# Attention score matmuls with 128 rows throughout: the queries' remainders in zero-padded tiles

## Chip, cores and metric

One core of one Trainium2 chip (trn2). The metric is the device time of the program in microseconds (us), the median over runs of the same kernel on the chip. PE stands for TensorE's matmuls, PEld for its weight loads, DVE for VectorE, ACT for ScalarE, POOL for GpSimd, SP for SyncE.

## What is computed

Two layers of a transformer over 512 latent tokens (and 256 context tokens) of width 1024, in float32: feed-forward, mixer, feed-forward. The mixer of layer 0 is a pooling one, that of layer 1 is a differential attention with 8 heads, each with two halves of 64 columns. Only the attention is touched here:

```python
def proj(h):                      # queries, keys: 8 heads x 2 halves x 64; values: 8 heads x 128
    q, k, v = jnp.split(h @ w_qkv, 3, axis=-1)
...
def attend(q, k, v):
    s = jnp.einsum('bqhjd,bkhjd->bhjqk', q, k).astype(jnp.float32) * scale
    p = jax.nn.softmax(s, axis=-1)
    a = p[:, :, 0] - lam_full * p[:, :, 1]
    return jnp.einsum('bhqk,bkhe->bqhe', a.astype(v.dtype), v)
```

The 512 latent queries see 768 keys (latents and context). Each of the two halves of a head has its own scores and its own softmax; the second softmax is subtracted from the first.

## The kernel before

Everything that goes through TensorE is float32 split into a high part and a rest (type fp32r), so that a product of two numbers takes three matmuls: high by high, high by rest, rest by high (`mm3`, L556 to L559). A weight's item of 512 columns is cast by ACT (L155) and its rest is taken by DVE (L156), six items ahead of their use.

The program runs in stages: feed-forward, pooling, feed-forward, feed-forward, attention, feed-forward with the final norm. The attention (L1170 to L1481) goes through 32 steps s, four blocks of 128 queries for each of the 8 heads, written out as a loop at L1437. Step s puts this on the queues, in this order: `combine(s-1)`, which joins the two softmaxes of the step before on DVE (L1302); three transposes of the joined block of step s-2 on PE (L1324), which ACT and DVE split again (L1326, L1327); `score(s, 0)`; three more transposes; `score(s, 1)`; then pieces of other work that a table spreads over the steps (projections of queries, keys and values of later heads, named `pj`; the output projection `yo`); and, in odd steps, the product with the values (`pv`).

`score(s, j)` (L1281) makes the scores of half j of a head for 128 queries and 768 keys, in two matmul pairs of 384 keys. The contraction has only 64 rows, and the other 64 of the 128 partitions carry the keys' rest: `k0` holds the high part of half 0's keys in partitions 0 to 63 and their rest in 64 to 127, `k1` the other way round (`k_split`, L1216). `q0` and `q1` hold the queries' high part twice. So one 128-row matmul (L1291) gives high by high plus high by rest. The queries' own rest lies in one tile `ql`, half 0 in partitions 0 to 63, half 1 in 64 to 127 (L1241, L1242), and a second matmul with 64 rows (L1292) multiplies it with the keys' high part:

```python
nc.tensor.matmul(o, q[:, qs], k[:, ks], start=True, stop=False)
lately["pe"] = nc.tensor.matmul(o, ql[rows, qs], k[rows, ks], start=False, stop=True).ins
```

There are 64 such scores, so 128 matmuls of each line. What follows a score: DVE takes the maximum (L1294, L1295), ACT the exponentials with their sums (L1298). Scores lie in two PSUM tiles used in turn. The queries are turned by `rope` (L1198), whose two POOL operations (L1205, L1206) stand ahead of the split of the queries (L1237 to L1242) and of the keys (L1219 to L1222).

`sT` (L87), the silu of the conditioning vectors, is 1 KB in each partition of a pool that lives through the whole program; it is read in the modulation vectors' matmuls and sums (L391, L398).

Of the kernel before, what the change touches and what calls it, by code (L numbers as in the profile page):

```python
# [11 lines left out]
F32 = mybir.dt.float32  # L12
F32R = mybir.dt.float32r
# [5 lines left out]
P = 128  # L19
D = 1024  # L20
KD = D // P
NL = 512
# [10 lines left out]
# how far the weights' items, their raw tiles and the units of the vectors' weights run ahead  # L33
# [3 lines left out]
# vectors that the tensor engine does as a whole; vectors done by the end of each stage; units between other work  # L37
# [12 lines left out]
class Half:  # L50
    """Half of the tokens in the order lat, ctx; segs: (residual tile, first column, columns, conditioning, offset)."""
# [8 lines left out]
def dit_kernel(ctx: ExitStack, tc: tile.TileContext, a: dict, out: bass.AP):  # L60
    nc = tc.nc
# [25 lines left out]
    sT = base.tile([P, KD, 32], F32, name="sT")  # L87
# [19 lines left out]
    # ---------------------------------------------------------------- weight stream  # L107
    # Raw tiles come by DMA; items of 512 columns are split from them into a high part and the rest, in the order
    # in which the tensor engine asks for them.
# [55 lines left out]
    def weights(key, keep=False):  # L165
        """The two parts of an item; the splitting of the following ones is emitted first."""
        n = item_of[key]
        issue(n + 1 + (AHEAD if state["ahead"] else 0))
        return split[n] if keep else split.pop(n)
# [7 lines left out]
    sums = {}  # L177

    def pre(c, which):
        """Sums of the four blocks of a chunk (gate, up) x (first, second half of d)."""  # L180
        def f(raws):
            g, u = raws[0], raws[1]
            g0, g1, u0, u1 = g[:, 0:512], g[:, 512:1024], u[:, 0:512], u[:, 512:1024]
            if which == "S1":
                return sums.pop((c, "S1"))
            t = stemp()
            if which == "S2":
                s1 = stemp()
                nc.gpsimd.tensor_add(s1, u0, u1)  # L189
                sums[(c, "S1")] = s1  # L190
                nc.gpsimd.tensor_sub(t, s1, g0)
                sums[(c, "S2")] = t
                return t
            if which == "S3":
                nc.gpsimd.tensor_sub(t, g0, u0)
                return t
            nc.gpsimd.tensor_sub(t, g1, sums.pop((c, "S2")))  # L197
            return t
        return f
# [39 lines left out]
    def plan_cols(key, w, rows):  # L239
        """Items of two row blocks by 256 columns each."""  # L240
        for m in range(0, rows, 4):
            r = raw_job(lambda t, m=m: nc.sync.dma_start(
                t[:, 0:256 * min(4, rows - m)].rearrange("p (k f) -> p k f", f=256), w[:, m:min(m + 4, rows)]))
            for e in range(min(4, rows - m) // 2):
                add_item(key + (m // 2 + e,), [r], half(e))
# [10 lines left out]
    # products: weights block, normed block  # L256
# [24 lines left out]
    # ---------------------------------------------------------------- background work, drained between matmuls  # L281
# [11 lines left out]
    # ---------------------------------------------------------------- modulation vectors  # L293
# [37 lines left out]
    class Ada:  # L331
        """The vectors' weights come as units of 128 rows and 512 columns. A vector's products with the two rows of
        silu are either summed over the units first, per partition, so that the tensor engine has only the sums of
        the partitions left, or are the tensor engine's as a whole."""
# [15 lines left out]
        def room(self, u):  # L350
            """The tag that takes unit u: the sums' places take one too as long as no sum is near."""
# [54 lines left out]
        def tick(self, count):  # L406
            """The next units, up to the limit."""
# [29 lines left out]
        def until(self, n):  # L437
            """Vectors that are to be through before the next limit."""
            self.limit = n * 2 * KD
# [9 lines left out]
    # ---------------------------------------------------------------- norms  # L449
# [14 lines left out]
    def norm_square(pool, h, k, eng):  # L464
        """Adds chunk k of x*x to the half's accumulator; the last one is kept apart."""
# [12 lines left out]
    def rstd_of(pool, st, nb, count):  # L478
        """1/sqrt(mean + eps) of sums that lie with the tokens on the partitions."""
# [16 lines left out]
    def spread(diag, ps, nb):  # L496
        """Tokens from the partitions to the free axis, the same on every partition."""
        nc.tensor.matmul(ps[:, 0:nb * P], ones, diag[:, 0:nb * P], start=True, stop=True)

    def stat_steps(pool, bank, h, keep=True):  # L500
        """The two steps of a half's norm; other matmuls may go between them."""
# [26 lines left out]
    def scaled(pool, h, k, l, i, dst):  # L528
        """x * rstd * g * (1 + scale), before the shift."""
# [14 lines left out]
    def direct(pool, h, k, l, i, place, t=None):  # L544
        """Both parts of the modulated chunk; place(seg) says where they go."""
# [15 lines left out]
    # ---------------------------------------------------------------- feed-forward  # L561
    class FFN:
        """x += gate/2 * swiglu(hn), in chunks of 128 hidden units that are summed into x two at a time.

        Gate and up of a chunk are the two row blocks of a 2x2x2 block product (halves of d, halves of the tokens),
        done with seven block products (Strassen-Winograd) instead of eight."""
# [11 lines left out]
        # normed blocks and their sums  # L578
# [16 lines left out]
        def first_half(self, k):  # L595
            """Plain blocks of the first half; their values before the split are kept for the sums."""
# [16 lines left out]
        def pair_mod(self, j):  # L613
            """Modulated second half of d chunks j, j+4."""
# [7 lines left out]
        def pair_first(self, j):  # L622
            """The second half's blocks that the plain products of d chunks j and j+4 need, and T3."""
# [17 lines left out]
        # seven products of a chunk  # L641
# [12 lines left out]
        def use(self, c, name, ps):  # L654
            """What follows a product; t, u, s, v: running sums of chunk c."""
# [43 lines left out]
        # second product  # L699
        def y_k(self, b, k, h, c0):  # L700
            """Sum k into x for the tokens of h, which lie from column c0 on."""
# [33 lines left out]
        def first(self, lead, between=None, each=None):  # L735
            """Chunks 0 and 1, block by block; lead() brings the second half's norm on its way. between() goes between
            the two chunks' products of the first half; each(j) brings the first half's d chunks j and j+4. Returns
            what comes last."""
# [96 lines left out]
        def finish(self, each, steps, halves=None):  # L835
            """The last sum into x, half by half; each(half, k, m) follows a chunk's sum. steps: the two steps of the
            first half's norm, given once that half is through; what they queue is drained behind the chunks."""
# [15 lines left out]
    # ---------------------------------------------------------------- start  # L853
# [8 lines left out]
    fp1 = stage.enter_context(tc.tile_pool(name="fp1", bufs=1, reuse_waits="tile"))  # L862

    class Both:
        """Tiles of the feed-forward phases: fp1 from the start on, fp2 once the start is through."""
# [12 lines left out]
    with tc.tile_pool(name="st", bufs=1, reuse_waits="tile") as st:  # L878
# [10 lines left out]
        # rows k of the d blocks; columns j, j+4 of shift and of scale  # L889
# [10 lines left out]
        def more(n):  # L900
            """The next n loads of tokens and of the first two vectors' weights, in the order of need."""
# [92 lines left out]
    # ---------------------------------------------------------------- layer 0 and the first half of layer 1  # L994
# [10 lines left out]
    # pooling mixer, each token set with zeros on both sides  # L1005
# [101 lines left out]
    def lead(f, m, keep=True, queue=True):  # L1107
        """The steps of half m's norm for f; the first half's blocks are queued behind them."""
# [33 lines left out]
    # the normed tokens for the attention, lat then ctx  # L1142
    hn = {}
# [26 lines left out]
    # ---------------------------------------------------------------- differential attention  # L1170
# [45 lines left out]
    def k_split(kt, src, cols):  # L1216
        """Keys of both halves of a head: each half as high part and rest, one on top of the other."""
# [7 lines left out]

    def piece_q(h):
        qt = [ap.tile([P, NL], F32R, name=f"q{n}", tag=f"q{n}", bufs=2) for n in range(3)]
# [6 lines left out]
    def split_q(h):  # L1234
        t1 = turned.pop((h, 0))
        q0, q1, ql = qkt[h][0]
# [4 lines left out]
        nc.vector.tensor_sub(ql[LO_], t1[LO_], q0[LO_].bitcast(F32))  # L1241
        nc.vector.tensor_sub(ql[HI_], t1[HI_], q1[HI_].bitcast(F32))  # L1242
# [33 lines left out]
    def later(f, *args):  # L1276
        """f's work behind the latest scores and softmax."""
# [3 lines left out]
    def score(s, j):  # L1281
        h, qt = divmod(s, 4)
        qs = slice(qt * P, (qt + 1) * P)
        rows = (LO_, HI_)[j]
        (q0, q1, ql), (k0, k1) = qkt[h]
        q, k = ((q0, k0), (q1, k1))[j]
        sc = pp.tile([P, 2, 512], F32, name="sc", tag="sc", bufs=2)
        for half in range(2):
# [3 lines left out]
            lately["pe"] = nc.tensor.matmul(o, ql[rows, qs], k[rows, ks], start=False, stop=True).ins  # L1292
# [9 lines left out]
    def combine(s):  # L1302
        """p0 - lambda Z0/Z1 p1; the division by Z0 is part of the norm that follows the weighted sum."""
# [41 lines left out]
    def sub_rstd(ha, hb):  # L1345
        """osum <- 1/sqrt(mean(o*o) + eps*Z0*Z0) for heads ha..hb-1, o taken before the division by Z0."""
# [136 lines left out]
    # ---------------------------------------------------------------- last feed-forward, final norm  # L1483
# [15 lines left out]
    def turn(g, q, b):  # L1499
        """Quarter q of the rows of block b of the half, as token-major columns."""  # L1500
# [7 lines left out]
    def gained(g, b, half):  # L1508
        """The columns times the gain, before the row's factor."""
# [95 lines left out]
```

## Time and profile before

| | before |
|---|---|
| median of 3 runs (lowest to highest) | 2545.51 us (2544.54 to 2546.41) |
| span of the profiled execution | 2547.6 us |
| mean granted TensorE clock | 0.979 of full speed |
| PE busy | 2448.8 us (96%) |
| PEld busy | 2283.7 us (90%) |
| DVE busy | 2251.2 us (88%) |
| ACT busy | 1053.1 us (41%) |
| POOL busy | 698.2 us (27%) |
| DMA | 240.95 MB, 95 GB/s on average |

The page gives the span of the profiled execution, from its first to its last instruction, and no other time of that execution; the span stands 2.1 us above the median of the runs. A matmul's row begins when the instruction is taken up, and its length includes the time in which it is in the pipe, so that rows of neighbours overlap: what a matmul costs is read from the distance between the starts of neighbours. A PE that is busy throughout is therefore not a PE at its peak.

### The profile page before, as it was taken

What the parts mean: (1) busy time and instruction counts of PE and PEld (TensorE: products, weight loads), DVE (VectorE), ACT (ScalarE), POOL (GpSimd) and SP (SyncE); (2) the same over time, 40 slices, a digit from 0 to 9 for tenths busy, and PEclk for the clock granted to TensorE, in tenths of its full rate; (3) what the DMA queues carried; (4) which work ended last, traced back from release to release, by engine and by line L of the source; (5) the groups of instructions that cost most, each with busy time, mean ns of one, the idle gap of its engine ahead of it and who ended that gap; (6) DMA issues with size and microseconds to landing.
All of it is one profiled execution on the core that took longest, in us unless ns stands there. A gap on an engine that the chain in (4) does not pass through costs nothing.

```text
span 2547.6 us, 41218 instructions
## 1 busy us (share of the span) xinstructions
PE 2448.8 (96%) x15159; PEld 2283.7 (90%) x15159; DVE 2251.2 (88%) x4094; ACT 1053.1 (41%) x2082; POOL 698.2 (27%) x556
## 2 busy tenths in 40 slices
PE   8999999998899999999899999999999999899998
PEld 5899999996689999999899999998787778899998
DVE  5998999998998889989899999997777777899998
ACT  4533333334543333334533323335555554544444
POOL 0422222225432222222422222222312201433332
PEclk7999999998899999999999999999999999999999
DMA  9434333333323233333123334331111112232332
GB/s 265 124 104 120 104 112 121 112 116 108 96 65 106 84 99 92 100 108 91 50 86 118 112 108 121 116 92 59 50 38 38 34 34 83 67 96 88 100 100 67
DMA packets 314822, 240.95 MB, mean 95 GB/s; under 512 B 11293, under 2 KB 278910, under 8 KB 314622
## 3 DMA queue, kind: packets, MB, share of 16 engines
q1 hardware_dynamic: 314336, 238.20, 31.4%
q8 instruction: 121, 1.98, 0.3%
q14 instruction: 79, 0.65, 0.1%
q10 hardware_dynamic: 286, 0.12, 0.0%
HBM read 236.18 MB, written 2.10 MB: 94 GB/s over the span
## 4 chain that ended last, share of the span: by engine, by line
PE 64%; DVE 22%; issue 6%; DMA 4%; ACT 3%; POOL 2%; DVEq 0%; ACTq 0%; SPq 0%; POOLq 0%
PE prod L558 10%; PE prod L557 10%; PE prod L559 10%; PE y L557 6%; PE y L558 6%; PE y L559 6%; DVE asum L402 5%; DVE wlo L156 4%; DMA wrs<-in_ffn_w_out 3%; DVE hn L542 2%; PE sc L1292 2%; DVE xl L711 2%; DVE tmp L692 1%; PE pj L557 1%; PE sc L1291 1%
## 5 line engine op out<-in xcount | busy, mean ns | idle before, releaser
L558 PE MATMUL prod<-hn,whi 128*128 128x384 f32 (+1 forms) x2496 | 810.6, 325 | 17.3 <-DVE hn L542 17.2
L557 PE MATMUL prod<-hn,whi 128*128 128x384 f32 (+1 forms) x2496 | 808.6, 326 | 9.7 <-ACT hn L541 7.8
L559 PE MATMUL prod<-hn,wlo 128*128 128x384 f32 (+1 forms) x2496 | 809.0, 324 | 2.8 <-DVE wlo L156 2.7
L558 PEld LDWEIGHTS prod<-hn,whi 128*128 128x128 f32 x2496 | 475.7, 191 | 23.0 <-DVE hn L542 22.3
L557 PEld LDWEIGHTS prod<-hn,whi 128*128 128x128 f32 x2496 | 474.0, 191 | 24.0 <-ACT hn L541 11.5
L557 PE MATMUL y<-h_hi,whi 128*128 128x384 f32 (+2 forms) x1408 | 463.5, 329 | 24.4 <-DVE tmp L669 13.7
L559 PEld LDWEIGHTS prod<-hn,wlo 128*128 128x128 f32 x2496 | 475.5, 191 | 4.9 <-DVE wlo L156 4.1
L558 PE MATMUL y<-h_lo,whi 128*128 128x384 f32 (+2 forms) x1408 | 459.9, 327 | 5.2 <-DVE h_lo L542 5.1
L559 PE MATMUL y<-h_hi,wlo 128*128 128x384 f32 (+2 forms) x1408 | 456.4, 324 | 0.0
L155 ACT CAST whi<-ws 128x512 fp32r<-128x512 f32 x320 | 195.4, 619 | 485.9 <-PE y L558 361.1
L711 DVE SCALAR_TENSOR_TENSOR xl<-y,mT,xl 128x384 f32<-128x384 f32 (+3 forms) x688 | 311.8, 481 | 17.6 <-PE y L559 17.4
L402 DVE SCALAR_TENSOR_TENSOR asum<-araw,sT,asum 128x512 f32<-128x512 f32 x364 | 317.6, 885 | 0.4 <-ACT asum L400 0.2
L197 POOL TENSOR_TENSOR ws<-wraw,ws 128x512 f32<-128x512 f32 x80 | 111.6, 1394 | 728.3 <-DVE wlo L156 728.3
L557 PEld LDWEIGHTS y<-h_hi,whi 128*128 128x128 f32 x1408 | 266.7, 190 | 45.0 <-DVE tmp L669 18.9
L156 DVE TENSOR_TENSOR wlo<-wraw,whi 128x512 fp32r<-128x512 f32 x336 | 282.4, 845 | 23.7 <-ACT whi L155 23.2
L558 PEld LDWEIGHTS y<-h_lo,whi 128*128 128x128 f32 x1408 | 265.9, 189 | 10.9 <-DVE h_lo L542 9.1
L155 ACT CAST whi<-wraw 128x512 fp32r<-128x512 f32 x340 | 205.0, 617 | 164.0 <-PE y L558 61.1
L559 PEld LDWEIGHTS y<-h_hi,wlo 128*128 128x128 f32 x1408 | 266.2, 189 | 2.0 <-issue 0.5
L156 DVE TENSOR_TENSOR wlo<-ws,whi 128x512 fp32r<-128x512 f32 x320 | 247.8, 775 | 9.4 <-ACT whi L155 7.8
L189 POOL TENSOR_TENSOR ws<-wraw 128x512 f32<-128x512 f32 x80 | 114.1, 1426 | 396.7 <-DMA wraw<-in_ffn_w_in 317.5
L156 DVE TENSOR_TENSOR wlo<-wrs,whi 128x512 fp32r<-128x512 f32 x176 | 144.3, 822 | 62.4 <-ACT whi L155 62.0
L155 ACT CAST whi<-wrs 128x512 fp32r<-128x512 f32 x176 | 106.8, 618 | 196.6 <-DMA wrs<-in_ffn_w_out 160.8
(257 smaller groups left out, 3632.9 us busy)
## 6 DMA issues: line engine op xcount, KB each, us to landing
wraw<-in_ffn_w_in SPq DMA_DIRECT2D x176, 512.0 KB, 4.0
araw<-in_ada_w SPq DMA_DIRECT2D x246, 256.0 KB, 2.7
wrs<-in_ffn_w_out SPq DMA_DIRECT2D x176, 256.0 KB, 3.1
wraw<-in_diff_w_qkv SPq DMA_DIRECT2D x24, 512.0 KB, 3.7
hn<-in_ada_w SPq DMA_DIRECT2D x32, 256.0 KB, 5.3
asum<-in_ada_w SPq DMA_DIRECT2D x10, 256.0 KB, 2.8
hn<-in_x SPq DMA_DIRECT2D x8, 256.0 KB, 3.6
wraw<-in_diff_w_o SPq DMA_DIRECT2D x4, 512.0 KB, 4.0
```

The source lines that it names most:

```text
L155: nc.scalar.copy(hi, src)
L156: (nc.gpsimd if n in by_pool else nc.vector).tensor_sub(lo, src, hi.bitcast(F32))
L189: nc.gpsimd.tensor_add(s1, u0, u1)
L197: nc.gpsimd.tensor_sub(t, g1, sums.pop((c, "S2")))
L402: nc.vector.scalar_tensor_tensor(to, raw, by, to, op0=ALU.mult, op1=ALU.add)
L542: (eng or nc.vector).tensor_sub(dst[1], src, dst[0].bitcast(F32))
L557: nc.tensor.matmul(ps, whi, hi, start=start, stop=False)
L558: nc.tensor.matmul(ps, whi, lo, start=False, stop=False)
L559: nc.tensor.matmul(ps, wlo, hi, start=False, stop=stop)
L692: nc.vector.tensor_mul(up, up, gate)
L711: self.latest = nc.vector.scalar_tensor_tensor(x[:, k, t0:t0 + n], ps[:, off:off + n], mT[self.l][:, self.gate_v, k, cond:cond + 1], x[:, ...
L1292: lately["pe"] = nc.tensor.matmul(o, ql[rows, qs], k[rows, ks], start=False, stop=True).ins
```

## The change

The queries' rest gets a tile of its own for each half of a head: `l0` has half 0's rest in partitions 0 to 63 and zeros in 64 to 127, `l1` zeros below and half 1's rest above. Two pairs of such tiles serve the heads in turn. Their zero halves are written once, by four POOL memsets at the beginning of the attention, and only the other halves are written again for each head. The second matmul of a pair then uses all 128 rows of the padded tile and of the keys' tile; the zeros remove the keys' rest. `sT` moves into a pool that ends with the feed-forwards before the attention. Comments are taken out as well, so lines in the changed kernel stand one lower up to the attention and five or six higher in it.

```diff
-    sT = base.tile([P, KD, 32], F32, name="sT")
...
     fp1 = stage.enter_context(tc.tile_pool(name="fp1", bufs=1, reuse_waits="tile"))
+    sT = fp1.tile([P, KD, 32], F32, name="sT")
...
+    rests = [[apool.tile([P, NL], F32R, name=f"ql{j}{m}") for j in range(2)] for m in range(2)]
+    for pair in rests:
+        nc.gpsimd.memset(pair[0][HI_].bitcast(F32), 0.0)
+        nc.gpsimd.memset(pair[1][LO_].bitcast(F32), 0.0)
+
     def piece_q(h):
-        qt = [ap.tile([P, NL], F32R, name=f"q{n}", tag=f"q{n}", bufs=2) for n in range(3)]
+        qt = [ap.tile([P, NL], F32R, name=f"q{n}", tag=f"q{n}", bufs=2) for n in range(2)] + rests[h % 2]
...
-        q0, q1, ql = qkt[h][0]
+        q0, q1, l0, l1 = qkt[h][0]
...
-        nc.vector.tensor_sub(ql[LO_], t1[LO_], q0[LO_].bitcast(F32))
-        nc.vector.tensor_sub(ql[HI_], t1[HI_], q1[HI_].bitcast(F32))
+        nc.vector.tensor_sub(l0[LO_], t1[LO_], q0[LO_].bitcast(F32))
+        nc.vector.tensor_sub(l1[HI_], t1[HI_], q1[HI_].bitcast(F32))
...
-        rows = (LO_, HI_)[j]
-        (q0, q1, ql), (k0, k1) = qkt[h]
-        q, k = ((q0, k0), (q1, k1))[j]
+        (q0, q1, l0, l1), (k0, k1) = qkt[h]
+        q, ql, k = ((q0, l0, k0), (q1, l1, k1))[j]
...
-            lately["pe"] = nc.tensor.matmul(o, ql[rows, qs], k[rows, ks], start=False, stop=True).ins
+            lately["pe"] = nc.tensor.matmul(o, ql[:, qs], k[:, ks], start=False, stop=True).ins
```

The order of PE's instructions stays. This is PE in step 2 of the attention before, the transposes and the two scores of a step (sizes are those of the output, so the 64 rows of L1292 do not show in them):

```order
L1324 MATMUL atr<-ident,p 128x128 x3
L1291 MATMUL sc<-k_18696,q_18693 128x384
L1292 MATMUL sc<-k_18696,q_18695 128x384
L1291 MATMUL sc<-k_18696,q_18693 128x384
L1292 MATMUL sc<-k_18696,q_18695 128x384
L1324 MATMUL atr<-ident,p 128x128 x3
L1291 MATMUL sc<-k_18697,q_18694 128x384
L1292 MATMUL sc<-k_18697,q_18695 128x384
```

And the same place in the changed kernel:

```order
L1329 MATMUL atr<-ident,p 128x128 x3
L1296 MATMUL sc<-k_18703,q_18701 128x384
L1297 MATMUL sc<-k_18703,ql_18530 128x384
L1296 MATMUL sc<-k_18703,q_18701 128x384
L1297 MATMUL sc<-k_18703,ql_18530 128x384
L1329 MATMUL atr<-ident,p 128x128 x3
L1296 MATMUL sc<-k_18704,q_18702 128x384
L1297 MATMUL sc<-k_18704,ql_18531 128x384
```

Every second matmul of a pair reads one of two padded tiles where both read the one tile of the rest before; nothing stands elsewhere.

On POOL, at the seam between the feed-forward and the attention, four instructions are new. In brackets stand the engines that an instruction waits for. Before:

```order
L476 TENSOR_TENSOR acc<-acc,tmp 128x256 [waits Activation_49,Pool_49] x4
L1205 TENSOR_TENSOR t_18730<-t_18730,sin_t 128x512 [waits DVE_49,DMAHW6_49,PE_49,Activation_49]
L1206 TENSOR_TENSOR t_18731<-t_18731,t_18730 128x512 [waits PE_49,Pool_49]
L1239 TENSOR_SCALAR q_18693<-t_18731 64x512 [waits Pool_49]
L1240 TENSOR_SCALAR q_18694<-t_18731 64x512
```

And in the changed kernel:

```order
L475 TENSOR_TENSOR acc<-acc,tmp 128x256 [waits Activation_49,Pool_49] x4
L1229 MEMSET ql_18530 64x512 [waits DVE_49,PE_49,Pool_49]
L1230 MEMSET ql_18531 64x512
L1229 MEMSET ql_18532 64x512
L1230 MEMSET ql_18533 64x512 [waits DVE_49]
L1205 TENSOR_TENSOR t_18737<-t_18737,sin_t 128x512 [waits DVE_49,DMAHW6_49,Activation_49,Pool_49]
L1206 TENSOR_TENSOR t_18738<-t_18738,t_18737 128x512 [waits Pool_49]
L1245 TENSOR_SCALAR q_18701<-t_18738 64x512 [waits Pool_49]
```

The memsets stand between the last sum of squares of the stage before and the first rope multiplication, and take over a wait for PE that this multiplication had. On DVE and ACT the order is unchanged.

## Rows read from the trace of the kernel before

**Rows 1.** The page, part 4: the chain that ended last, share of the span by engine.

```profile
PE 64%; DVE 22%; issue 6%; DMA 4%; ACT 3%; POOL 2%; DVEq 0%; ACTq 0%; SPq 0%; POOLq 0%
```

**Rows 2.** Stretches of the attention: engines' busy us (instructions), PE clock, DMA share, GB/s.

```profile
core 0: us, PE busy (x) PEld busy (x) DVE busy (x) ACT busy (x) POOL busy (x), PEclk, DMA share, GB/s
1791.10:1822.20 31.10, 29.51 (x135) 21.20 (x134) 26.51 (x51) 19.07 (x37) 9.09 (x6) 0.92 0.18 53
...
1833.80:1883.90 50.10, 50.10 (x279) 39.72 (x277) 39.01 (x77) 28.67 (x59) 16.23 (x12) 1.00 0.14 41
1883.90:1917.50 33.60, 33.60 (x216) 28.11 (x213) 19.91 (x40) 14.65 (x31) 0.00 (x0) 1.00 0.12 35
...
2001.20:2054.90 53.70, 53.70 (x288) 41.17 (x285) 44.73 (x86) 28.69 (x59) 17.00 (x12) 1.00 0.10 30
...
2065.00:2112.10 47.10, 47.10 (x258) 36.24 (x257) 35.28 (x73) 25.83 (x52) 0.00 (x0) 1.00 0.15 45
```

**Rows 3.** Weight loads of the scores, 1788 to 2110 us: busy, mean ns, idle before, releasers.

```profile
L1291 PEld LDWEIGHTS sc<-k,q 128*128 128x128 f32 x128 | 24.5, 191 | 14.0 <-issue 12.2 <-ACT p L1298 0.7 <-DVE k L1221 0.4
...
L1292 PEld LDWEIGHTS sc<-k,q 64*128 64x128 f32 x128 | 23.8, 186 | 25.1 <-issue 25.1
```

**Rows 4.** Timeline of PE in step 10: start us, length us, instruction.

```profile
1883.64 0.49 PE L1324 MATMUL atr<-ident,p 128*128 128x128 f32 x3
1883.89 0.42 PE L1291 MATMUL sc<-k,q 128*128 128x384 f32 x1
1884.24 0.44 PE L1292 MATMUL sc<-k,q 64*128 64x384 f32 x1
1884.62 0.44 PE L1291 MATMUL sc<-k,q 128*128 128x384 f32 x1
1884.99 0.44 PE L1292 MATMUL sc<-k,q 64*128 64x384 f32 x1
1885.36 0.55 PE L1324 MATMUL atr<-ident,p 128*128 128x128 f32 x3
1885.66 0.42 PE L1291 MATMUL sc<-k,q 128*128 128x384 f32 x1
...
1887.12 0.39 PE L1268 MATMUL pj<-whi,hn 128*128 128x256 f32 x1
1887.34 0.28 PE L1269 MATMUL pj<-wlo,hn 128*128 128x256 f32 x1
1887.46 0.29 PE L1270 MATMUL pj<-whi,hn 128*128 128x256 f32 x1
```

**Rows 5.** Timeline of PE in a feed-forward: first and last of 14 neighbours.

```profile
1599.66 0.34 PE L558 MATMUL y<-h_lo,whi 128*128 128x384 f32 x1
...
1601.93 0.34 PE L559 MATMUL y<-h_hi,wlo 128*128 128x384 f32 x1
```

**Rows 6.** Timeline of POOL at the seam to the attention; in brackets idle time and releaser.

```profile
1748.93 4.64 POOL L476 TENSOR_TENSOR acc<-acc,tmp 128x256 f32<-128x256 f32 x5 [3.53 <-ACT tmp L462]
1779.56 1.49 POOL L1205 TENSOR_TENSOR t<-t,sin_t 128x512 f32<-128x512 f32 x1 [25.99 <-PE pj L1270]
...
1784.06 1.80 POOL L1240 TENSOR_SCALAR q<-t 64x512 fp32r<-64x512 f32 x1
```

**Rows 7.** The same columns as rows 2, a feed-forward and the pooling stage.

```profile
598.00:660.00 62.00, 48.97 (x377) 33.09 (x377) 53.80 (x99) 30.23 (x62) 31.06 (x27) 0.73 0.46 141
...
1500.00:1600.00 100.00, 98.37 (x566) 95.37 (x565) 99.41 (x176) 34.93 (x67) 25.85 (x17) 1.00 0.39 117
```

**Rows 8.** PE in step 3: the wait (timeline) and the stretch behind it (columns of rows 2).

```profile
1813.38 0.88 PE L1324 MATMUL atr<-ident,p 128*128 128x128 f32 x6 [1.15 <-DVE mx L1295]
...
1820.00:1824.00 4.00, 4.00 (x16) 3.01 (x14) 1.36 (x3) 1.27 (x4) 0.00 (x0) 0.50 0.02 4
```

## Prediction

> **What bounds the kernel now.** I read the page's chain first: PE carries 64% of what ended last, DVE 22% [rows 1]. That is a mean over the stages, so the attention is read by itself, in stretches [rows 2]. From the first score (1791 us) to the end of the last score's step (2112 us) PE is busy for the whole of every stretch but the first, while DVE has between 19.91 of 33.60 us (59%) and 26.51 of 31.10 us (85%). PE is the bound there, and a microsecond taken from PE comes off the end as long as DVE keeps up.
>
> What does PE do in that time? The weight loads show it: of the 128 loads of the 64-row matmuls each follows idle time, 25.1 us in all, 0.196 us each, that nothing but "issue" ended, and those of the 128-row score matmuls have another 12.2 us of the same kind [rows 3]. No semaphore is waited for. Then the timeline of PE [rows 4]: from a 128-row score matmul to the 64-row one behind it, or back, 0.37 us pass, for 384 columns. In a feed-forward, where all neighbours have 128 rows, the same 384 columns take (1601.93 - 1599.66) / 13 = 0.175 us [rows 5], at the same full clock. So a change between the two kinds of matmul costs about 0.195 us, which is just the length of a weight load (186 to 191 ns) [rows 3]: the next weights are loaded only when the matmul ahead is through, where they would otherwise come in beside it.
>
> **The change part by part.** *The score matmuls.* A score has four matmuls, and four changes of kind: three between them and one to whatever follows. From its first start to the start of what follows it takes 1885.36 - 1883.89 = 1.47 us, and the second score of the step 1887.12 - 1885.66 = 1.46 us [rows 4]. With one kind, 4 x 0.175 = 0.70 us. The saving is 0.77 us a score, over 64 scores 49.3 us. The neighbour behind a score pays too: three transposes take 1885.66 - 1885.36 = 0.30 us behind one and 1883.89 - 1883.64 = 0.25 us behind a projection, and the first projection matmul behind the second score takes 0.22 us where the next takes 0.12 us [rows 4]. Over 32 steps that is 32 x (0.05 + 0.10) = 4.8 us. **Gross: 54.1 us, 1.69 us a step.** That a zero row costs as much as any other is taken from the columns: 64-row and 128-row loads have the same length [rows 3], and I give a matmul with zeros the 0.175 us of rows 5.
>
> *What DVE gives back.* DVE's work stays the same, so each stretch can shrink only to what DVE needs. By stretches [rows 2], with 1.69 us off each step:
> - 1791.1 to 1822.2, 4 steps: PE would need 24.3 us, DVE has 26.5 us of work.
> - 1833.8 to 1883.9, 5 steps (a stretch of the same kind follows at 1917.5): 41.6 us against 39.0.
> - 1883.9 to 1917.5, 3 steps (another at 1967.6): 28.5 against 19.9, no question.
> - 2001.2 to 2054.9, 5 steps: 45.2 against 44.7.
> - 2065.0 to 2112.1, 5 steps: 38.6 against 35.3.
>
> How full can DVE get? In a feed-forward it is busy 99.41 of 100 us while PE still has 98.37; in the pooling stage, where DVE and its short chains set the pace, 53.80 of 62 us, 87% [rows 7]. I take 95%, nearer to the first, because the attention's parts are a step apart (a block is transposed two steps after its scores, and a projection or two lies between a score and the values' product), which is the kind of slack that the feed-forward has and the pooling stage lacks. Then the first stretch ends at 26.5 / 0.95 = 27.9 us, 3.6 later than PE alone would; the fourth at 47.1, 1.9 later; for the second, the one like it and the fifth, where PE still needs more than DVE, I put 0.5 us each for single waits. **Given back: 7.0 us.** At 99% it would be 2.5 us, at 87% it is (30.5 - 24.3) + 2 x (44.8 - 41.6) + (51.4 - 45.2) + (40.6 - 38.6) = 20.8 us; both ends are kept for the range.
>
> *The four memsets.* The nearest rows for a POOL pass over 64x512 are those of the copy of the queries, up to 1.80 us; four make 7.2 us [rows 6]. They stand behind the last sum of squares, which ends at 1753.57 us, and ahead of the first rope multiplication, which begins at 1779.56 after 25.99 us of idleness [rows 6]. That idleness hides them: cost nothing. They wait for readers of the memory that they take over, all of the stage before, so I see them through well before 1779. If they were released only then, the rope multiplication, and with it the first head's queries, would come up to 7.2 us later; below nothing they can't cost, as nothing was taken off POOL.
>
> *The rest.* DVE's two subtractions of a head's rest keep their size and place, and only write elsewhere. `sT` moves without an instruction; the tiles behind it lie a little differently, so that a few waits on earlier owners of the memory sit on other instructions: nothing, as the owners are of the stage before. Around 1820 us PE runs at half clock [rows 8], for about two steps; if a change of kind costs twice as much there, 16 x 0.195 = 3.1 us come on top of the gross sum. I leave that for the range.
>
> **The sum.** 54.1 - 7.0 = 47.1 us off the profiled span of 2547.6 us gives 2500.5. The median of the runs stands 2.1 us lower than that span, so for the median 2498.4: **I forecast 2499 us.** Without any loss to DVE and with the half-clock extra it would be 2488; with DVE filled to 87% only, 2512.
>
> **One rule against it.** The starts of neighbours with 128 rows are 0.175 us apart although each has a load of 0.19 us [rows 3, 5], so a load does run beside the matmul ahead of it when both use all rows. The Trainium skill, "TensorE: Matmul & The Clock Gate", section "Part 3: Packing small matmuls", states the opposite: a weight load overlaps with a matmul in flight only when the two are in different row groups. By that rule padding would make every pair conflict and bring nothing. The trace disagrees with it (0.175 us against the 0.37 that load and matmul would take one after the other); the rule is the second rival below.
>
> **The rivals.**
> - *DVE becomes the bound.* Its queue is strictly in order, and maximum, exponential, joining, transposing and splitting form a chain over three engines; with PE faster, single waits at 1 us could turn up in every step, as the one of 1.15 us in step 3 [rows 8]. For it: today's shares of 75 to 85% in the work-heavy stretches [rows 2] leave little room. Against it: PE has no gap at all in the stretches behind 1833 us [rows 2]. With 87% it is 2512, and were DVE to reach only 80%, the first stretch and that at 2001 would gain nothing, the second and the one like it 1.3 us each, the last 3.0, and the two light ones (5.1 each) and two single steps outside the list (1.7 each) all of theirs: 19 us, 2526. So 2505 to 2530.
> - *The pairs stay 0.37 us apart.* If the distance came from something else that both matmuls share (the same output, the same keys), it would stay: 2545, no change. Against it: a feed-forward's three matmuls share an output as well and keep 0.175 us [rows 5].
> - *The clock falls: slower.* In step 3 PE waited 1.15 us for DVE, and soon after it was granted 0.50 [rows 8], 1.2 GHz. In the pooling stage, where PE waits for DVE again and again, the clock is 0.73 over 62 us [rows 7], so about 54% of that time is spent at half speed. If the attention, freed of its padding time, came to run like that over its 275 us, 148 us would be at half speed and cost half of that, 74 us, against the 47 gained: 2572. The point at which it decides is 94 us at half clock, a third of the attention. For it: PE will wait more than today. Against it: PE keeps 100% of the clock from 1834 to 2112 us [rows 2], and its matmuls get denser.
>
> **How the numbers follow.** A measurement of this kernel tells about 0.2% (5 us) from no change. Forecast (2488 to 2505): 0.70. DVE as the bound (2505 to 2530): 0.23, of which two thirds lie below 2516. Pairs unchanged: 0.03. Clock: 0.04, half of it slower, the other half split between no change and a small gain. Faster: 0.70 + 0.23 + 0.01 = 0.94; same: 0.03 + 0.01 = 0.04; slower: 0.02. The range 2488 to 2516 holds the forecast and the better part of the first rival, 0.85, with the rest for sums that are off.
>
> **What would show it.** In the changed kernel's timeline the score matmuls should start 0.17 to 0.18 us apart, the idle time put down to "issue" before their loads should be gone, and from the first score to the end of the last step some 274 us should pass in place of 321, with DVE busy for about 87% of them. The stretches around steps 0 to 3 and 21 to 25 should be those where PE waits for DVE. The memsets should lie in the idle time before 1779 us. If the score matmuls are 0.175 us apart and the attention still takes over 300 us, the DVE term was wrong; if they are 0.37 us apart, the reading of the cause was; if the granted clock is 0.5 for more than 20 us behind 1834 us, the clock is what I missed.

## The result and the profile after

| | before | changed |
|---|---|---|
| median of 4 runs each, same chip | 2545.96 us | 2501.91 us (2500.58 to 2504.59) |
| ratio to before, 95% interval | | 0.9831 (0.9817 to 0.9845) |
| span of the profiled execution | 2547.6 us | 2498.8 us |
| first score to last output-projection matmul (`yo`) | 361.0 us | 314.4 us |
| ahead of the first score | 1791.1 us | 1787.9 us |
| behind the last output-projection matmul | 395.6 us | 396.5 us |

The change takes 44 us off, 1.7%. The two profiled executions are 48.8 us apart: 46.5 us in the attention and 3.2 us ahead of it, less 0.9 us behind it. The 3.2 us are no part of the change: two kernels of this study that differ from the kernel before in the scores alone (the reordered ones with 64 rows, below) start their first score at 1787.2 and 1787.6 us, and all ten profiles lie between 1786.3 and 1791.8 us.

Spans and medians have to be kept apart here. In every run on record that has both numbers, the time is 1.7 to 1.9 us more than the span of the same execution. By that, the span of 2547.6 us before goes with a time of some 2549.4 us, 3.4 us above the median beside it and above every time of the kernel before on record (2539.6 to 2546.8 us). So the 48.8 us between the two spans are more than the change is worth.

The page of the changed kernel, its busy times and its chain, which still names PE first [rows 1 before]:

```profile
PE 2393.7 (96%) x15159; PEld 2275.9 (91%) x15159; DVE 2243.7 (90%) x4094; ACT 1050.6 (42%) x2082; POOL 699.8 (28%) x560
...
PE 67%; DVE 18%; issue 5%; DMA 4%; ACT 3%; POOL 2%; DVEq 0%; ACTq 0%; SPq 0%; POOLq 0%
```

PE's busy time fell by 55.1 us with the same 15159 matmuls, DVE's by 7.5 us with the same instructions.

The timeline of PE in step 14 of the attention (start us, length us, instruction). Rows 4 show step 10 of the kernel before, with the same transposes and scores:

```profile
1903.28 0.49 PE L1329 MATMUL atr<-ident,p 128*128 128x128 f32 x3
1903.53 0.42 PE L1296 MATMUL sc<-k,q 128*128 128x384 f32 x1
1903.78 0.34 PE L1297 MATMUL sc<-k,ql 128*128 128x384 f32 x1
1903.96 0.34 PE L1296 MATMUL sc<-k,q 128*128 128x384 f32 x1
1904.13 0.34 PE L1297 MATMUL sc<-k,ql 128*128 128x384 f32 x1
1904.31 0.49 PE L1329 MATMUL atr<-ident,p 128*128 128x128 f32 x3
1904.55 0.42 PE L1296 MATMUL sc<-k,q 128*128 128x384 f32 x1
...
1905.33 0.28 PE L556 MATMUL pj<-hn,whi 128*128 128x256 f32 x1
1905.45 0.28 PE L557 MATMUL pj<-hn,whi 128*128 128x256 f32 x1
```

Score matmuls start 0.17 to 0.18 us apart, but for the first one behind the transposes, from which 0.25 to 0.26 us pass to the next. The projection behind the second score starts its next matmul after 0.12 us in place of 0.22. The weight loads (lines view, 1780 to 2060 us: busy, mean ns, idle before) have lost the idle time that nothing but "issue" ended, 25.1 and 12.2 us before [rows 3]:

```profile
L1297 PEld LDWEIGHTS sc<-k,ql 128*128 128x128 f32 x128 | 24.3, 190 | 0.1
L1296 PEld LDWEIGHTS sc<-k,q 128*128 128x128 f32 x128 | 24.1, 188 | 2.5 <-ACT p L1303 1.2 <-DVE k L1221 0.6 <-issue 0.5
```

The stretches of the same steps as in rows 2:

```profile
core 0: us, PE busy (x) PEld busy (x) DVE busy (x) ACT busy (x) POOL busy (x), PEclk, DMA share, GB/s
1787.90:1814.20 26.30, 21.86 (x135) 18.99 (x134) 25.31 (x50) 19.07 (x37) 9.07 (x6) 1.00 0.21 63
1814.20:1822.30 8.10, 8.06 (x42) 6.56 (x41) 7.51 (x17) 4.97 (x11) 0.00 (x0) 1.00 0.08 23
1822.34:1864.88 42.54, 42.54 (x279) 39.45 (x278) 38.33 (x77) 28.07 (x58) 16.30 (x12) 1.00 0.17 49
1864.88:1893.90 29.02, 29.02 (x216) 27.91 (x214) 19.64 (x41) 14.66 (x32) 0.00 (x0) 1.00 0.18 51
...
1965.40:2014.20 48.80, 46.66 (x288) 40.83 (x286) 43.49 (x86) 28.48 (x59) 17.10 (x12) 1.00 0.10 33
...
2022.80:2063.90 41.10, 41.10 (x270) 37.39 (x269) 35.48 (x75) 26.59 (x54) 0.00 (x0) 1.00 0.16 52
```

From the first score to the end of the last step 276.0 us pass, where the prediction has some 274, and DVE is busy for 233.4 us of them, 85% (forecast about 87%). PE has gaps in the first stretch (steps 0 to 3) and in that from 1965 to 2014 us (steps 21 to 25), and in no other of length. Its waits in the attention, 1.3 us in two rows before, are now 6.7 us; the three longest:

```profile
PE atr L1329 <- DVE p L1314: 2.1, 1, 2.1
PE pv L557 <- DVE aT_lo L1332: 1.9, 2, 1.0
PE orstd L497 <- DVE diag L491: 1.3, 1, 1.3
```

The memsets lie in POOL's idle time ahead of the first rope multiplication [rows 6 before], 0.52 us each:

```profile
1756.35 0.52 POOL L1229 MEMSET ql<- 64x512 f32 x1 [5.65 <-DVE hn L553]
...
1758.05 0.52 POOL L1230 MEMSET ql<- 64x512 f32 x1
1776.36 1.48 POOL L1205 TENSOR_TENSOR t<-t,sin_t 128x512 f32<-128x512 f32 x1 [17.79 <-DVE t L1204]
```

### The profile page after: what moved, and what is told of

Its sections match the earlier page's. It is cut to its first block, busy times and chain, and to the rows that moved or that the text cites. A ratio compares the mean times of both kernels' runs of the same rounds, so it can differ in the third digit from the quotient of the medians.

```text
span 2498.8 us, 41221 instructions
## 1 busy us (share of the span) xinstructions
PE 2393.7 (96%) x15159; PEld 2275.9 (91%) x15159; DVE 2243.7 (90%) x4094; ACT 1050.6 (42%) x2082; POOL 699.8 (28%) x560
## 4 chain that ended last, share of the span: by engine, by line
PE 67%; DVE 18%; issue 5%; DMA 4%; ACT 3%; POOL 2%; DVEq 0%; ACTq 0%; SPq 0%; POOLq 0%
PE prod L556 11%; PE prod L557 11%; PE prod L558 11%; PE y L556 7%; PE y L557 7%; PE y L558 7%; DVE asum L401 3%; DMA wrs<-in_ffn_w_out 3%; DVE wlo L155 3%; DVE hn L541 2%; ACT whi L154 1%; PE pj L556 1%; PE pj L557 1%; PE pj L558 1%; DVE h_hi L530 1%
```

## The experiments

In what follows the attention's length is again that from the first score to the last output-projection matmul, in the profile of each kernel. Theory A is that of the prediction: what costs is the change between a 128-row and a 64-row matmul. The first four ran beside a kernel before of 2543.71 us, 2.3 us less than in the result above, so the times expected for them are to be read as that much lower.

**Everything but the rows.**

```diff
+        rows = (LO_, HI_)[j]
...
-            lately["pe"] = nc.tensor.matmul(o, ql[:, qs], k[:, ks], start=False, stop=True).ins
+            lately["pe"] = nc.tensor.matmul(o, ql[rows, qs], k[rows, ks], start=False, stop=True).ins
```

> Everything of the change stays (four padded tiles, four memsets, sT in its new place), but the second matmul of a pair reads only the 64 rows that are not zero, as before. Theory A (each change between a 128-row and a 64-row matmul costs some 0.2 us, and nothing else of the edit matters): the pairs go back to 0.37 us apart and the time to 2544 to 2548 us, that is all of the 44 us is lost. Rival (part of the gain comes from where tiles lie and what waits for them, or the memsets cost something): it stops short of that or goes beyond it, 2530 to 2540 us or over 2550.

Measured: 2542.95 us against 2543.71 for the kernel before on that chip, ratio 0.9999 (0.9990 to 1.0009). The whole gain is gone; the tiles, the memsets and `sT`'s place are worth nothing either way, to some 2.5 us. Step 14 takes 7.28 us again, as before (7.30). The idle time put down to "issue" is back (waits of the weight loads, 1780 to 2100 us: total, times, longest):

```profile
PEld sc L1298 <- issue: 24.4, 128, 0.3
PEld sc L1297 <- issue: 11.9, 64, 0.2
```

**Half the scores padded.** In the changed kernel the second matmul of half 1 takes its 64 rows only:

```diff
+        rows = (slice(0, P), HI_)[j]
...
-            lately["pe"] = nc.tensor.matmul(o, ql[:, qs], k[:, ks], start=False, stop=True).ins
+            lately["pe"] = nc.tensor.matmul(o, ql[rows, qs], k[rows, ks], start=False, stop=True).ins
```

> The changed kernel, but half 1 of each head uses 64 rows again and half 0 all 128. Theory A (cost per change of kind, four in each score): half of the gain stays, 2523 to 2526 us, with half 0's matmuls 0.175 us and half 1's 0.37 us apart. Rival (DVE paces the attention already, PE has room): much more than half stays, under 2515 us. Rival (the clock or a queue switches as a whole): under a quarter stays.

Measured: 2520.67 us, ratio 0.9912 (0.9898 to 0.9927): 23 us off, half of the gain. On PE's timeline both kinds stand in one step:

```profile
1913.19 0.42 PE L1297 MATMUL sc<-k,q 128*128 128x384 f32 x1
1913.45 0.34 PE L1298 MATMUL sc<-k,ql 128*128 128x384 f32 x1
1913.63 0.34 PE L1297 MATMUL sc<-k,q 128*128 128x384 f32 x1
...
1914.57 0.44 PE L1298 MATMUL sc<-k,ql 64*128 64x384 f32 x1
1914.94 0.45 PE L1297 MATMUL sc<-k,q 128*128 128x384 f32 x1
```

0.18 us within half 0, 0.37 us within half 1. The gain goes with the number of changes, four a step in place of eight, so PE was the bound for nearly all of it.

**The same matmuls in another order.** The kernel before, with the two 128-row matmuls of a score ahead of its two 64-row ones:

```diff
             nc.tensor.matmul(o, q[:, qs], k[:, ks], start=True, stop=False)
+        for half in range(2):
+            ks = slice(half * 384, (half + 1) * 384)
+            o = sc[:, half, 0:384]
             lately["pe"] = nc.tensor.matmul(o, ql[rows, qs], k[rows, ks], start=False, stop=True).ins
```

> The kernel before, with the four matmuls of a score in another order: both 128-row ones, then both 64-row ones. Same matmuls, same rows, but two changes of kind in a score in place of four. Theory A (the change of kind costs): half of 4 x 0.195 us goes, neighbours of one kind are 0.175 us apart, and the time falls by some 22 to 25 us to 2521 to 2525 us. Rival B (a 64-row matmul is slow in itself, and so is what follows it): the 64-row ones stay 0.37 us apart and the time stays at 2543 to 2547 us. Rival C (64-row matmuls of the same rows cost nothing behind one another): under 2515 us.

Measured: 2520.08 us, ratio 0.9907 (0.9892 to 0.9922), 24 us off without a padded row. This is what tells theory A from rival B: the 64-row matmuls are all there, half of the changes are not. PE in step 14:

```profile
1912.86 0.49 PE L1327 MATMUL atr<-ident,p 128*128 128x128 f32 x3
1913.10 0.59 PE L1291 MATMUL sc<-k,q 128*128 128x384 f32 x2
1913.62 0.61 PE L1295 MATMUL sc<-k,q 64*128 64x384 f32 x2
1914.16 0.55 PE L1327 MATMUL atr<-ident,p 128*128 128x128 f32 x3
```

Two 64-row matmuls take 0.54 us from their first start to that of the transposes. The 0.54 - 2 x 0.175 = 0.19 us above the price of two matmuls belong to two changes: the later half of the one into 64 rows and the earlier half of the one out of them. A change so costs 0.19 us in all, and nothing else is slow about 64 rows. The Trainium skill, "TensorEngine Tiling (Array Packing)", section "Tiling Modes", Key Properties, says that changing the tiling mode, not just the tile, drains TensorE. The traces agree in what costs: 0.19 us for a change between 128 and 64 rows, and none between the two halves of 64 rows (last experiment). That the engine drains in this time is seen in no row.

**The padded matmuls left out.** The changed kernel without the product of the queries' rest:

```diff
-            nc.tensor.matmul(o, q[:, qs], k[:, ks], start=True, stop=False)
-            lately["pe"] = nc.tensor.matmul(o, ql[:, qs], k[:, ks], start=False, stop=True).ins
+            lately["pe"] = nc.tensor.matmul(o, q[:, qs], k[:, ks], start=True, stop=True).ins
```

> The changed kernel without its padded matmuls: the product of the queries' rest with the keys is left out, 128 matmuls of 384 columns fewer, 128 x 0.175 = 22.4 us of PE. Theory A with DVE at 95% as a floor: the stretches of steps 0 to 3 and 21 to 25 gain nothing, the others what PE gives up or a little less: 13 to 16 us, 2486 to 2489 us. Rival (PE alone bounds the attention): the full 22 us, 2480 us. Rival (DVE is the bound by now): under 5 us, 2497 us or more.

Measured: 2492.14 us, ratio 0.9796 (0.9782 to 0.9811). The attention takes 306.7 us, 7.7 less than the changed kernel's, so a third of the 22.4 us of PE. The rest went into new waits of PE, 13.9 us in all where the changed kernel has 6.7, of which the longest three:

```profile
PE atr L1328 <- DVE p L1313: 3.5, 2, 2.7
PE sc L1296 <- ACT p L1302: 3.5, 4, 1.7
PE orstd L497 <- DVE mx L1299: 2.6, 1, 2.6
```

and into the clock, which falls beside these waits (columns as above; PEclk is the fourth number from the right):

```profile
1806.50:1812.50 6.00, 4.11 (x13) 3.06 (x14) 5.67 (x11) 3.94 (x8) 0.00 (x0) 0.53 0.00 1
1997.20:2000.50 3.30, 2.74 (x7) 1.61 (x8) 2.22 (x6) 1.14 (x3) 2.79 (x2) 0.62 0.02 5
```

Some 10 us run at 1.2 GHz there, which costs about 5 (an estimate, half of them). 7.7 + 7.2 + 5 make 19.9 of the 22.4 us. The expectation of theory A (13 to 16 us) was too good, and the time lies between it and the rival in which DVE is the bound. Steps 4 to 20 give 7.3 us and steps 26 to 30 give 3.0, but steps 0 to 3 and 21 to 25, which were to gain nothing, became longer by 1.5 and 1.7 us. The chain over DVE and ACT, and the half clock in these two stretches, hold more than a DVE filled to 95% does. How much of the half clock is due to this edit stays open, since the profile of before has as much of it (10.2 us).

**DVE relieved.** The changed kernel again, on one chip with the three kernels below it, and with 20 of the attention's weight rests on POOL:

```diff
+    by_pool.update(n for key, n in item_of.items() if key[0] == "qk" and key[1] > 0 and key[3] == 1
+                   or key[0] == "v" and key[1] > 0 and key[2] % 2 == 1)
```

> The changed kernel itself, on the chip of the runs beside it, as their measure: 42 to 46 us faster than the kernel before.

> The changed kernel with 20 of the attention's weight rests (L156; some 0.75 us each on DVE, 15 us in all) taken by POOL, which is idle for most of the attention. Theory A (what is left of waits for DVE costs some 5 us, above all in steps 0 to 3 and 21 to 25): 1 to 4 us faster than the changed kernel. Rival (DVE bounds the whole attention by now): 8 us or more faster. Rival (POOL is strictly in order and late with the queries' turning): slower by 3 us or more.

Measured: the changed kernel 2500.84 us, ratio 0.9827 (0.9812 to 0.9842); with the rests on POOL 2503.39 us, 0.9830 (0.9814 to 0.9847): no difference clear of the noise. Two of the expectations have it faster, which it is not; the third (slower by 3 us or more) can't be told from no change by medians 2.6 us apart. DVE has 9.6 us less to do from the first score to the start of the last step (216.9 in place of 226.5), but the attention takes 314.8 us against 314.4. A period of eight steps from the middle, first in the changed kernel, then with the rests on POOL:

```profile
1892.50:1964.10 71.60, 71.60 (x492) 67.40 (x490) 57.92 (x120) 45.25 (x92) 16.30 (x12) 1.00 0.15 45
```

```profile
1898.10:1969.70 71.60, 71.60 (x492) 67.39 (x490) 54.46 (x114) 45.26 (x92) 24.10 (x18) 1.00 0.15 45
```

PE alone sets this period. Steps 0 to 3 (26.7 us against 26.4) and 21 to 25 (48.7 both) are no shorter either, but here the run tells little: only 1.0 and 1.2 us of the 9.6 were taken out of these two stretches, and the first of them has 3.4 us at half clock with the rests on POOL (0.94 below) and none in the changed kernel:

```profile
1791.80:1818.50 26.70, 23.46 (x135) 20.25 (x134) 24.45 (x47) 18.56 (x36) 14.14 (x10) 0.94 0.27 80
```

Whether the amount of work on DVE sets their waits, or the order of the steps, was not settled.

**64 rows made cheap.** The kernel before, with both scores of a step together and the 64-row matmuls in turn from the two halves of the partitions; and the same order with padded tiles:

```diff
+    def scores(s):
...
+        for half in range(2):
+            for sc, rows, k in zip(both, (LO_, HI_), (k0, k1)):
+                lately["pe"] = nc.tensor.matmul(sc[:, half, 0:384], ql[rows, qs], k[rows, cols[half]], start=False, stop=True).ins
...
         if 0 <= u < 4 * HEADS:
             transpose(u, 1)
         if live:
-            score(s, 1)
+            scores(s)
```

> The kernel before with both scores of a step made together: four 128-row matmuls, then the four 64-row ones, in turn from partitions 0 to 63 and 64 to 127. The rule that padding gives something up: matmuls in different row halves run beside each other, so two of them take little more than one, and PE needs some 4 x 0.175 + 2 x 0.175 + 2 x 0.2 = 1.45 us a step for scores: within 3 us of the same order with padded tiles (next run), although it has two changes of kind. If they run one after the other at 0.175 us: 0.4 us a step, 13 us, slower than the padded one. If going from one half to the other is a change of kind as well: five changes a step, 1.0 us, some 32 us slower than the padded one.

> The changed kernel in the order of the run before this one: the control. No change of kind in either order, so the same PE time as the changed kernel; both scores of a step now wait for both PSUM tiles to be free: the same as the changed kernel to 8 us slower.

Measured: 2510.95 us, ratio 0.9866 (0.9851 to 0.9881), with 64 rows; 2503.63 us, 0.9839 (0.9824 to 0.9853), padded, 2.8 us above the changed kernel as expected. So 64-row matmuls can come within 7 us of the padded ones, not within the 3 us expected. PE in step 14, first with 64 rows:

```profile
1908.36 0.94 PE L1289 MATMUL sc<-k,q 128*128 128x384 f32 x4
1909.23 0.62 PE L1292 MATMUL sc<-k,q 64*128 64x384 f32 x4
1909.78 0.39 PE L557 MATMUL pj<-hn,whi 128*128 128x256 f32 x1
```

then padded:

```profile
1903.71 0.94 PE L1295 MATMUL sc<-k,q 128*128 128x384 f32 x4
1904.49 0.86 PE L1298 MATMUL sc<-k,ql 128*128 128x384 f32 x4
1905.18 0.28 PE L556 MATMUL pj<-hn,whi 128*128 128x256 f32 x1
```

Four 64-row matmuls take 0.55 us with the change in it, four padded ones 0.69. Their weight loads show why (PEld, the same place): four loads of 0.183 to 0.187 us are through in 0.30 us, two at a time.

```profile
1909.23 0.30 PEld L1292 LDWEIGHTS sc<-k,q 64*128 64x128 f32 x4 [0.25 <-issue]
```

Matmuls of opposite halves run beside each other: within such a pair they start 3 ns apart or less in this step, and at most 10 ns in the steps that kept this order. The Trainium skill states it in "TensorE: Matmul & The Clock Gate", section "Part 3: Packing small matmuls", with a distance of some 4 ns; the trace agrees. Together with the two changes of kind the step comes out at 1.42 us plus 0.10 in what follows, against 1.47 us padded. In 6 of the 32 steps the order came apart (two and two in place of four and four), with four changes and no two matmuls beside each other. That is 0.8 us more for each of these steps, 4.8 us, as much as the two profiles' attentions are apart (324.6 and 319.6 us). Padding beats it by little and is simpler; neither order beats the change itself.

## Why the prediction was right

**The cause** was right: 0.37 us between neighbours is a change of kind, and it goes when all have 128 rows. The second rival, that the pairs stay 0.37 us apart, and the rule of the Trainium skill that the prediction set against itself ("TensorE: Matmul & The Clock Gate", section "Part 3: Packing small matmuls": a load overlaps only with a matmul of other row groups) are refuted by the 0.175 us between neighbours with loads of 0.19 us.

**The gross sum** was 54.1 us and is 48.7. Step 14 went from 7.30 us to 5.77, and steps 13 to 20, eight in a row in which PE has no gap, from 83.73 to 71.55: 1.52 us a step, not 1.69 (columns of rows 2, before and changed):

```profile
1917.46:2001.19 83.73, 83.73 (x492) 67.83 (x490) 59.29 (x120) 45.88 (x92) 16.21 (x12) 1.00 0.13 38
```

```profile
1893.90:1965.45 71.55, 71.55 (x492) 67.35 (x490) 57.94 (x120) 45.20 (x92) 16.31 (x12) 1.00 0.16 45
```

The term that was mis-sized is "4 x 0.175 = 0.70 us" for a score. It measures 1904.31 - 1903.53 = 0.78 us, as the first score matmul behind three transposes takes 0.25 us. Its row begins while the third transpose still runs: three transposes then one score matmul show 0.25 us for the former and 0.25 for the latter, in place of 0.33 and 0.17. Those 0.08 us were there before, too, inside the first 0.35 us, and I counted them as cost of a change. A plain count does better: 8 changes a step x 0.19 us = 1.52 us.

**What DVE gives back** was put at 7.0 us. PE's waits grew from 1.3 to 6.7 us, by 5.4, in the two stretches named. The first takes 26.3 us (27.9 forecast), that of steps 21 to 25 48.8 us (47.1). So the size was near, partly by luck, as an error of 1.6 us down in the one stretch met one of 1.7 us up in the other. The reason holds in part: DVE was filled to 96% in the first and only to 89% in the second, where its fill alone does not explain the waits.

**The half clock** I had left to the range with up to 3.1 us. It went altogether: the changed kernel has the full clock in the attention [rows 8 before: 0.50]. The kernel with 64 rows again (the first experiment) has 6.8 us less at half clock than the profile of before, with the same matmuls, and an attention of 358.0 us in place of 361.0: so 10.2 us of it cost before some 4.4 us (an estimate, 3.0 / 6.8 of 10.2). In the two profiles this gain made up for most of what the gross sum had too much: 48.7 + 4.4 - 5.4 = 47.7 us, and 46.5 are measured in the attention.

Most of that gain was in the one profile of before and not in the medians. The first experiment's profiled execution (2543.14 us) lies at the median of its runs (2542.95); from its attention of 358.0 us to the 314.4 are 43.6 us, which are the 44 of the medians. The 47.1 us forecast were 1.7 too few by the two spans and 3.0 too many by the medians. The step from the span to the median, "2.1 us lower", was wrong: the changed kernel's median stands 3.1 us above its profiled span of 2498.8 us. So the median's miss of only 2.9 us is in part luck, errors that offset each other: 5.4 us too much in the gross sum, against 1.6 us too much given back and some half clock gained that the sum did not have.

**The memsets** cost nothing, as forecast; they last 0.52 us where 1.80 was the bound. **The rivals**: DVE as the bound did not come, the median is 3 us above the forecast and 3 below where that rival began. The falling clock did not come: both profiles of the changed kernel have the full clock in the whole attention. In the other kernels of this study it is at half for 3.4 to 10.2 us there, far from the 94 us at which that rival would decide.

## What to carry to other kernels

Look for idle time ahead of weight loads that nothing but "issue" ends, and for starts of neighbours that are further apart than in a dense stretch: where matmuls of different row counts alternate, each change cost 0.19 us here, a little more than a whole 384-column matmul (0.175 us). Either give all of them the same rows, with zeros, or group them; half the changes gave half the gain. When PE gets shorter, look at which chain ends its waits before taking load off the other engine, since 9.6 us less work on DVE gained nothing here, and price a matmul that follows a transpose from other rows behind transposes. Before a forecast goes from one profiled span to a median, compare that span with the spans of other runs.

## What was not expected of the hardware

- 64-row matmuls from opposite halves of the partitions start within 3 ns of each other (10 ns at most) and their loads run in pairs, with nothing done for it but the order.
- A wait of PE does not by its length tell whether the clock falls. With the padded matmuls left out, waits of 1 to 3 us in steps 2 to 3 and 24 to 25 went with 0.53 and 0.62. In the kernel before a wait of 1.15 us in step 3 was followed by 10.2 us at half clock, but the changed kernel waits up to 2.1 us in steps 2 to 3 and keeps the full clock, in both its profiles.
- The time at half clock in the attention differs between executions of the same matmuls: 10.2 us in the profile of before, 3.4 us in the first experiment.
- A matmul's row that follows a transpose begins 0.08 us early, so that distances there are shared out wrongly between neighbours.
